# Moving the strip loads of a three-group encoder kernel from SyncE's queue to GpSimd's

## The chip, the cores and the metric

The kernel runs on one core of one Trainium2 chip. A core has five engines with a queue of instructions each: TensorE (PE in the profile; its weight loads are shown as PEld), VectorE (DVE), ScalarE (ACT), GpSimd (POOL) and SyncE (SP). Each engine takes its instructions strictly in the order of its queue and waits on semaphores for the others. Transfers run on 16 DMA engines that all queues share; an instruction in the queue of SP, ACT or POOL starts each transfer.

The metric is the device time of one execution in microseconds (us), as a median over runs; lower is better.

## What is computed

The reference is a trunk of two layers on 256 tokens of width 2048 (`x`) with 256 memory tokens (`mem`), all in float32. Cut to what matters here:

```python
for l in range(DEPTH):                                   # DEPTH = 2
    h = rmsnorm(x, norm_g[l])
    proj = h @ w_in[l]                                   # 2048 x 7168
    a_x, a_b, a_c, a_g, d_q, d_k, d_v, d_g, m_q, m_g = split(proj)
    y_a = short_gated_conv(a_x, a_b, a_c, ...) * silu(a_g)
    y_d = diff_attention(...) * silu(d_g)
    mkv = rmsnorm(mem, mem_norm_g[l]) @ w_mem_kv[l]      # 2048 x 1024
    mk, mv = rmsnorm(mkv[..., :512] by head, mem_k_norm_g[l]), mkv[..., 512:]
    y_m = memory_attention(rmsnorm(m_q by head), mk, mv) * silu(m_g)
    x = x + concat(y_a, y_d, y_m) @ w_out[l]
```

## The kernel before

Every large product is made of three matmuls on PE: each operand is split into a high part rounded to PE's fast float32 format and a low part that holds the rest (high times high, high times low, low times high). ACT makes the high part, DVE the low part. The left operand must have the 2048 input columns on the partitions, so `mem`, `x` and all that follows is also needed turned.

**The memory stage comes first.** It computes `mkv` of both layers, 32 steps `s` in all: layer `l = s // 16`, and chunk `k = s % 16` of 128 of the 2048 input rows. A step loads one 128x1024 tile of `w_mem_kv` (`Memory.load`, L783, four `raw` buffers, SP's queue), splits it with the norm's gain (`Memory.make`, L793 on ACT and L794 on DVE, four buffers), and does twelve 128x512 matmuls in two halves, keys and values (`Memory.times`, L818 through L311). The loop at L905 runs the steps in order; the last two and the first two of a layer go as a group. `beside(s)` (L866) puts other work beside the steps. After a layer's last steps ACT copies the keys out of the accumulators (`kraw`, L894) and the values (`mv`, L899).

**How `mem` and `x` are turned.** Chunks 0 to 7 of `mem` are turned by PE (`rows_T`, L628). Chunks 8 to 15 of `mem` (two quarters, `m.columns`, L830) and all four quarters of layer 0's `x` (`x_turned`, L655) go another way: `strips_by_rows` (L639) loads a quarter of 512 columns as eight transfers of 64 KB, 512 bytes to a row, into a tile `xt` of the pool tag `e`, which has two buffers; DVE turns the tile in 32x32 blocks (`turn_strips`, L651) into `xf`; `split_T` (L267 and L268 for `memT`, L270 and L271 for `xT` with the gain `gx`) makes the two parts of the chunks. These transfers are issued from SP's queue, four and four, with the loads of weights between them. For `x` the four quarters are begun beside the steps k = 1, 4, 7 and 10 of layer 1.

**Small constants** (`load_constants`, L98) come on POOL's queue: four lambda vectors, `norm_g` into `gx`, and nine pieces into `vb`, in three parts beside k = 11, 12 and 13 of layer 0, held back by a copied column of `ssm` (L102). `rest_of_constants` (L154) works them out beside k = 8 of layer 1. POOL's queue also carries the keys' way through DRAM (`keys`, L744 out and L745 back), once for each layer.

**The order** of all that carries `keep_in_program_order` or `pin` is the order in which the program writes it; the rest is placed by a scheduler that works on a simulated time line. Generators in `tasks` yield the number of steps after which they go on (`later`, `run_side`).

Behind the memory stage come the blocks of each layer: `block` (L315) loads `w_in` or `w_out` tile by tile (L297), splits it (L300 on ACT, L301 on DVE) and multiplies (L311). The first block of layer 0 begins when its accumulators are free, that is, when L894 has copied the last keys.

Of the kernel before, what the change touches and what calls it, by code (L numbers as in the profile page):

```python
# [18 lines left out]
P = 128  # L19
# [29 lines left out]
def encoder(ctx: ExitStack, tc: tile.TileContext, x, mem, norm_g, w_in, conv_w, conv_b,  # L49
# [21 lines left out]
    def nm(s):  # L71
        uid[0] += 1
        return f"{s}_{uid[0]}"
# [24 lines left out]
    def load_constants(part):  # L98

        pin = tc.keep_in_program_order  # L100
        if part == 0:
            pin(nc.gpsimd.tensor_copy(vb[:, 0:NT], ssm[0:64, :, 3]))  # L102
            pin(nc.gpsimd.memset(vb, 0.0))
            for j, v in enumerate((lq1, lk1, lq2, lk2)):
                pin(nc.gpsimd.dma_start(lam_in[:, j, :], on_all_rows(v)))
        else:
            if part == 1:
                pin(nc.gpsimd.dma_start(gx.rearrange("p (m j) -> p m j", j=QT),
                                        norm_g.rearrange("l (q p j) -> p (l q) j", p=P, j=QT)))
            for r0, v in vb_rows[(part - 1) * 4:part * 4]:  # L110
                n, w = v.shape
                for j in range(P // w):
                    pin(nc.gpsimd.dma_start(vb[r0:r0 + n, j * w:(j + 1) * w], v))


    zeros = tmp.tile([P, NB], mybir.dt.bfloat16, tag="eT", name="zeros")
    nc.vector.memset(zeros, 0.0)
# [102 lines left out]
    def later(g, n):  # L220
        due[id(g)] = chunk[0] + n
        return g
# [399 lines left out]
    def rows_T(src, k, n):  # L622

        pt = ps_t.tile([P, 2, SEQ], F32, tag="t", name=nm("pt"))
        for j in range(n):
            for t in range(NT):
                tc.keep_in_program_order(
                    nc.tensor.transpose(pt[:, j, t * P:(t + 1) * P], src(k + j, t), ident))  # L628
        return [pt[:, j, :] for j in range(n)]

    def strips_of(src):

        st = tmp.tile([P, SEQ // B, B * QT], F32, tag="e", name=nm("xt"))
        for b in range(NA):
            tc.keep_in_program_order(nc.sync.dma_start(
                st[b * B:(b + 1) * B], src[:, b * B * QT:(b + 1) * B * QT].rearrange("(n p) r -> p n r", p=B)))
        return st

    def strips_by_rows(src):  # L639

        st = tmp.tile([P, SEQ // B, B * QT], F32, tag="e", name=nm("xt"))
        for n in range(SEQ // B):
            tc.keep_in_program_order(nc.sync.dma_start(  # L643
                st[:, n], src[n * B:(n + 1) * B].rearrange("p (b r) -> b p r", b=NA)))
            if n == SEQ // B // 2 - 1:
                yield 1
        return st

    def turn_strips(st):
# [2 lines left out]
                                                     st.rearrange("p n (c j) -> p j n c", j=QT)))  # L652
        return whole

    def x_turned(dst, l, q, src):  # L655

        if l == 0:
            st = yield from strips_by_rows(src)
            yield 3
        else:  # L660
            st = strips_of(src)
            yield 2
        whole = turn_strips(st)
        yield
        for j in range(QT):
            split_T(dst, q * QT + j, whole[:, j], g_norm(l, q * QT + j), pin=True)
            if j % 2:
                yield
# [97 lines left out]
    class Memory:  # L766
# [61 lines left out]
                split_T(memT, q * QT + j, self.strips[q][:, j], None, pin=True)  # L828

        def columns(self, q):  # L830
            self.strips[q] = yield from strips_by_rows(mem[:, q * NB:(q + 1) * NB])

    mkT, mv, stm, away = [], [], [], []
    m = Memory()
# [25 lines left out]
    m.begin(1, 0, 0)  # L860
    m.begin(1, 1, 0)
    m.begin(1, 0, 1)
    m.make(2)
    m.split(2, rows_T(mem_columns, 2, 2))

    def beside(s):  # L866

        l, k = divmod(s, KT)
        if l == 0:
            if k in (3, 5):  # L870
                m.split(k + 1, rows_T(mem_columns, k + 1, 2))
            if k in (3, 6):
                tasks.append(later(m.columns({3: 2, 6: 3}[k]), 0))
            if k in (6, 9):
                mem_tokens({6: 2, 9: 3}[k] * NB, NB)
            if k in (6, 7, 10, 11):
                m.turned(2 if k < 10 else 3, k % 2)
            if k in (2, 4, 8, 11):
                mem_squares((2, 4, 8, 11).index(k))
            if k == 11:  # L880
                tasks.append(later(mem_stats(), 1))
            if k in (11, 12, 13):
                load_constants(k - 11)
        else:
            if k == 8:
                rest_of_constants()
            if k in (1, 4, 7, 10):
                q = k // 3
                tasks.append(later(x_turned(xT, 0, q, x[:, q * NB:(q + 1) * NB]), 1))

    def keep_keys(l):
        kraw = keep.tile([P, NT, NB], F32, tag="ga", name=nm("kraw"))
# [12 lines left out]
    while s < DEPTH * KT:  # L905
        l, k = divmod(s, KT)
        group = (s, s + 1) if k in (KT - 2, 0) else (s,)
        for i in group:
            beside(i)
        for i in range(s, group[-1] + 3):  # L910
            m.make(i)
        for half in range(2):
            for i in group:
                m.times(i, half)
            if k == KT - 2:
                (keep_keys, keep_values)[half](l)
        for i in group:
            for ahead in range(i + 1, i + 5):
                m.load(ahead)
            run_side(1)  # L920
        s = group[-1] + 1
# [201 lines left out]
```

## Time and profile before

| what | value |
|---|---|
| median of 3 runs | 940.33 us (939.9 to 941.63) |
| the profiled execution, as a run | 942.95 us |
| its span in the profile | 940.8 us |
| mean granted clock of TensorE | 0.995 |
| busy: PE, DVE, ACT, POOL | 924.4, 672.9, 494.7, 14.8 us |
| issues of L643 (strips) on SP | 48, of 64 KB each |
| issues from POOL's queue | 24: 4 lambda vectors, `norm_g`, 9 of `vb`, 8 of `kd`, 2 back |

The profile comes from one execution. A row of the time line gives the start, the duration, the engine, the line of the kernel, the operation, what it writes and reads, the number of instructions merged in the row, and in brackets how long the engine had been idle before and what ended that. `SPq` marks the issue of a transfer, not the transfer itself. Rows of the chain of waits give start, duration, and what held the end back at that time.

### The profile page before, as it was taken

How to read it: one execution, taken by the hardware profiler on the slowest of the kernel's cores; microseconds unless marked ns; L12 is line 12 of the kernel's file. 1: busy time of each engine (PE TensorE's matmuls, PEld its weight loads, DVE VectorE, ACT ScalarE, POOL GpSimd, SP SyncE). 2: the span in 40 equal slices, each digit the busy share in tenths (PEclk: the TensorE clock that was granted, in tenths of full speed). 3: DMA queues.
4: the chain of work that ended last, by engine and by line, in shares of the span. 5: the costliest groups of instructions: out<-in, count | busy, mean ns of one | idle time of the engine just before them, and what ended most of it. 6: DMA issues, size and time to landing. Idle time of an engine off the chain costs nothing.

```text
span 940.8 us, 12267 instructions
## 1 busy us (share of the span) xinstructions
PE 924.4 (98%) x4159; PEld 763.2 (81%) x4159; DVE 672.9 (72%) x1179; ACT 494.7 (53%) x751; POOL 14.8 (2%) x33
## 2 busy tenths in 40 slices
PE   9889799999999999999999999999999999999998
PEld 6678588888888888888888888888888888888886
DVE  5667687866789686556767766887898776558652
ACT  6554564568455454435555544568654554446331
POOL 0031010000000000000000000000000000000000
PEclk9999899999999999999999999999999999999999
DMA  7777887886677999998678866886888989988762
GB/s 256 236 218 214 295 266 216 235 242 208 181 222 197 245 265 244 248 273 246 208 245 256 259 198 186 232 259 186 245 222 221 253 224 246 254 238 238 221 210 81
DMA packets 250765, 216.09 MB, mean 230 GB/s; under 512 B 130266, under 2 KB 177160, under 8 KB 250704
## 3 DMA queue, kind: packets, MB, share of 16 engines
q1 hardware_dynamic: 248416, 211.86, 77.9%
q0 software_dynamic: 1120, 2.41, 1.0%
q10 hardware_dynamic: 1168, 1.07, 0.4%
q8 instruction: 32, 0.52, 0.2%
q14 instruction: 29, 0.24, 0.1%
HBM read 194.31 MB, written 20.97 MB: 229 GB/s over the span
## 4 chain that ended last, share of the span: by engine, by line
PE 89%; DMA 4%; ACT 3%; DVE 2%; issue 1%; SPq 0%; DVEq 0%; ACTq 0%
PE acc L311 84%; DMA raw<-in_w_mem_kv_dram 4%; PE po L451 2%; ACT hi L793 2%; DVE lo L794 1%; DVE xf L651 1%; PE s L604 1%; PE s L559 1%; PE s L558 1%; SPq L643 0%; ACT msq L718 0%; PE acc L807 0%; PE warm L122 0%; ACT memT L267 0%; ACT sq L368 0%
## 5 line engine op out<-in xcount | busy, mean ns | idle before, releaser
L311 PE MATMUL acc<-hi,xT 128*128 128x512 f32 x1792 | 563.1, 392 | 2.8 <-ACT kraw L894 2.8
L300 ACT CAST hi<-raw 128x1024 fp32r<-128x1024 f32 x288 | 302.7, 1052 | 346.2 <-PE acc L311 290.7
L301 DVE TENSOR_TENSOR lo<-raw,hi 128x1024 fp32r<-128x1024 f32 x288 | 351.6, 1222 | 184.9 <-ACT hi L300 180.1
L311 PEld LDWEIGHTS acc<-hi,xT 128*128 128x128 f32 x1792 | 337.8, 189 | 72.7 <-ACT kraw L894 3.2
L311 PE MATMUL acc<-lo,xT 128*128 128x512 f32 x896 | 350.1, 391 | 0.0
L311 PEld LDWEIGHTS acc<-lo,xT 128*128 128x128 f32 x896 | 169.0, 189 | 34.3
L311 PE MATMUL acc<-hi,yT 128*128 128x512 f32 x512 | 158.0, 389 | 0.0
L311 PEld LDWEIGHTS acc<-hi,yT 128*128 128x128 f32 x512 | 96.1, 188 | 19.9
L311 PE MATMUL acc<-lo,yT 128*128 128x512 f32 x256 | 99.6, 389 | 0.0
L311 PE MATMUL acc<-hi,memT 128*128 128x512 f32 x248 | 79.2, 399 | 6.4 <-ACT hi L793 4.0
L311 PEld LDWEIGHTS acc<-hi,memT 128*128 128x128 f32 x248 | 47.1, 191 | 18.0 <-ACT hi L793 5.7
L794 DVE SCALAR_TENSOR_TENSOR lo<-raw,cva,hi 128x1024 fp32r<-128x1024 f32 (+1 forms) x34 | 41.4, 1221 | 22.0 <-ACT hi L793 22.0
L311 PEld LDWEIGHTS acc<-lo,yT 128*128 128x128 f32 x256 | 48.0, 188 | 10.1
L311 PE MATMUL acc<-lo,memT 128*128 128x512 f32 x124 | 48.7, 400 | 2.1 <-DVE lo L794 1.8
L793 ACT ACTIVATE hi<-raw,cva 128x1024 fp32r<-128x1024 f32 (+1 forms) x34 | 36.7, 1097 | 24.1 <-DMA raw<-in_w_mem_kv_dram 20.5
L311 PEld LDWEIGHTS acc<-lo,memT 128*128 128x128 f32 x124 | 23.7, 191 | 9.2 <-DVE lo L794 4.5
L569 ACT ACTIVATE e<-e,mx 128x256 f32<-128x256 f32 x48 | 23.8, 499 | 1.4 <-DVE mx L565 1.3
L651 DVE STREAM_TRANSPOSE xf<-xt 128x1024 f32<-128x1024 f32 x10 | 20.0, 2004 | 3.6 <-DMA raw<-in_w_mem_kv_dram 3.2
L270 ACT ACTIVATE xT<-xf,gx 128x256 fp32r<-128x256 f32 x32 | 14.5, 500 | 8.6 <-DVE xf L651 6.6
L413 DVE STREAM_TRANSPOSE sh<-sh 128x1024 f32<-128x1024 f32 (+2 forms) x14 | 17.3, 1234 | 0.0
L563 DVE SCALAR_TENSOR_TENSOR e<-dist,s 128x512 f32<-128x512 f32 x24 | 15.7, 678 | 2.2 <-PE s L559 1.7
L1084 DVE TENSOR_TENSOR xs<-acc,xs 128x256 f32<-128x256 f32 (+1 forms) x24 | 10.8, 503 | 7.8 <-PE acc L311 7.8
(159 smaller groups left out, 543.4 us busy)
## 6 DMA issues: line engine op xcount, KB each, us to landing
raw<-in_w_in_dram SPq DMA_DIRECT2D x192, 512.0 KB
raw<-in_w_out_dram SPq DMA_DIRECT2D x64, 512.0 KB
raw<-in_w_in_dram SPq DMA_DIRECT2D x64, 256.0 KB
raw<-in_w_mem_kv_dram SPq DMA_DIRECT2D x30, 512.0 KB
d<-sh SPq DMA_DIRECT2D x80, 128.0 KB
sh<-d SPq DMA_DIRECT2D x64, 128.0 KB
d<-yn SPq DMA_DIRECT2D x40, 64.0 KB
yn<-d SPq DMA_DIRECT2D x40, 64.0 KB
```

Of the source, the lines that this page charges most:

```text
L270: both = (nc.scalar.activation(hi, src, AF.Copy, scale=gain), nc.vector.scalar_tensor_tensor(lo, src, gain, hi.bitcast(F32), ALU.mult, ALU ...
L300: nc.scalar.copy(hi, raw)
L301: nc.vector.tensor_tensor(lo_, raw, hi.bitcast(F32), ALU.subtract)
L311: i = nc.tensor.matmul(acc, left, right, start=start, stop=stop)
L413: tc.keep_in_program_order(nc.vector.transpose(src, src))
L451: nc.tensor.matmul(po[:, t, :], eT[:, i, t, k, :], v[:, k, h * P:(h + 1) * P], start=k == 0, stop=k == NT - 1)
L563: nc.vector.scalar_tensor_tensor(e[:, c], dist, -slopes[h], s[c], ALU.mult, ALU.add)
L569: nc.scalar.activation(e[:, c, i], e[:, c, i], AF.Exp, bias=mx[:, c, i:i + 1], accum_out=sm[:, c, i:i + 1])
L651: tc.keep_in_program_order(nc.vector.transpose(whole.rearrange("p j (n i) -> p j n i", i=B), st.rearrange("p n (c j) -> p j n c", j=QT)))
L793: both = (nc.scalar.activation(hi[:, j], raw[:, j], AF.Copy, scale=g), nc.vector.scalar_tensor_tensor(lo[:, j], raw[:, j], g, hi[:, j].bit ...
L794: nc.vector.scalar_tensor_tensor(lo[:, j], raw[:, j], g, hi[:, j].bitcast(F32), ALU.mult, ALU.subtract))
L1084: nc.vector.tensor_tensor(xc, acc[t][:, lo:lo + n], xc, ALU.add)
```

## The change

1. `strips_by_rows` issues its eight transfers from POOL's queue, without a break after four. It can be given `after`: POOL then first copies one column of that tensor into the tile, and since the transfers write the same tile, they wait for the copy, which waits for its source.
2. The two quarters of `mem` wait in this way for one chunk of `memT` (chunk 5 for quarter 2, chunk 9 for quarter 3); quarter 3 is begun beside k = 7 and not 6. The first quarter of `x` waits for the memory's statistics (`stm`); the others have no copied column.
3. The quarters of `x` are begun beside k = 2, 3, 6 and 9 of layer 1 (before 1, 4, 7, 10), with waits of 3, 5, 5 and 5 steps until they are turned, so that the turning stands beside k = 5, 8, 11 and 14.
4. `norm_g` is loaded by a function of its own beside k = 9 of layer 0, held back by a copied column of `ssm`. The other constants come beside k = 4, 5 and 6 of layer 1, behind the first two quarters of `x` on POOL's queue, without a copied column; `rest_of_constants` goes from k = 8 to k = 11.
5. At the start, chunk 2's split of weights and the turning of chunks 2 and 3 stand within step 1 and not ahead of it, and step 1 makes the weights of steps 1 and 2 alone.

In the order that results, ACT has, ahead of the last copy of keys (`kraw`), the third cast of `w_in` and four `xT` casts; the scaling of `mkT` comes later than the copy. DVE has the last transpose of `x` behind the seventh split of `w_in` tiles.

```diff
@@ load_constants
         if part == 0:
-            pin(nc.gpsimd.tensor_copy(vb[:, 0:NT], ssm[0:64, :, 3]))
             pin(nc.gpsimd.memset(vb, 0.0))
...
-            if part == 1:
-                pin(nc.gpsimd.dma_start(gx.rearrange("p (m j) -> p m j", j=QT),
-                                        norm_g.rearrange("l (q p j) -> p (l q) j", p=P, j=QT)))
...
+    def load_norm():
+
+        tc.keep_in_program_order(nc.gpsimd.tensor_copy(gx[:, 0:NT], ssm[:, :, 1]))
+        tc.keep_in_program_order(nc.gpsimd.dma_start(gx.rearrange("p (m j) -> p m j", j=QT),
+                                                     norm_g.rearrange("l (q p j) -> p (l q) j", p=P, j=QT)))
...
-    def strips_by_rows(src):
+    def strips_by_rows(src, after=None):
 
         st = tmp.tile([P, SEQ // B, B * QT], F32, tag="e", name=nm("xt"))
+        if after is not None:
+            tc.keep_in_program_order(nc.gpsimd.tensor_copy(st[:, 0, 0:1], after))
         for n in range(SEQ // B):
-            tc.keep_in_program_order(nc.sync.dma_start(
+            tc.keep_in_program_order(nc.gpsimd.dma_start(
                 st[:, n], src[n * B:(n + 1) * B].rearrange("p (b r) -> b p r", b=NA)))
-            if n == SEQ // B // 2 - 1:
-                yield 1
         return st
...
-    def x_turned(dst, l, q, src):
-
-        if l == 0:
-            st = yield from strips_by_rows(src)
-            yield 3
-        else:
-            st = strips_of(src)
-            yield 2
+    def x_turned(dst, l, q, src, after=None, wait=2):
+
+        st = strips_of(src) if l else strips_by_rows(src, after)
+        yield wait
...
         def columns(self, q):
-            self.strips[q] = yield from strips_by_rows(mem[:, q * NB:(q + 1) * NB])
+            self.strips[q] = strips_by_rows(mem[:, q * NB:(q + 1) * NB], memT[:, 0, 4 * q - 3, 0:1].bitcast(F32))
...
     m.begin(1, 0, 1)
-    m.make(2)
-    m.split(2, rows_T(mem_columns, 2, 2))
...
-            if k in (3, 6):
-                tasks.append(later(m.columns({3: 2, 6: 3}[k]), 0))
+            if k in (3, 7):
+                m.columns({3: 2, 7: 3}[k])
...
+            if k == 9:
+                load_norm()
             if k == 11:
                 tasks.append(later(mem_stats(), 1))
-            if k in (11, 12, 13):
-                load_constants(k - 11)
         else:
-            if k == 8:
+            if k in (4, 5, 6):
+                load_constants(k - 4)
+            if k == 11:
                 rest_of_constants()
-            if k in (1, 4, 7, 10):
+            if k in (2, 3, 6, 9):
                 q = k // 3
-                tasks.append(later(x_turned(xT, 0, q, x[:, q * NB:(q + 1) * NB]), 1))
+                tasks.append(later(x_turned(xT, 0, q, x[:, q * NB:(q + 1) * NB], stm[0][:, R, 0:1] if q == 0 else None,
+                                            (3, 5, 5, 5)[q]), 0))
...
-        for i in range(s, group[-1] + 3):
+        for i in range(s, group[-1] + (2 if s == 1 else 3)):
             m.make(i)
         for half in range(2):
             for i in group:
                 m.times(i, half)
+            if s == 1 and half == 0:
+                m.split(2, rows_T(mem_columns, 2, 2))
```

## The prediction

> **What bounds the kernel now.** I read the page's first lines, then busy time by stretch, then the waits on TensorE (PE), and last the SyncE queue (SP) in the stretches where PE stood still.
>
> ```profile
> span 940.8 us, 12267 instructions
> PE 924.4 (98%) x4159; PEld 763.2 (81%) x4159; DVE 672.9 (72%) x1179; ACT 494.7 (53%) x751; POOL 14.8 (2%) x33
> ```
>
> PE sets the end, so an edit to transfers can only win where PE stands still or runs slowly. The view of stretches finds those places. Its columns: stretch, length, then busy time and instruction count of PE, PEld, DVE, ACT and POOL, granted clock, DMA share, GB/s.
>
> ```profile
> 31.40:45.20 13.80, 11.51 (x49) 8.86 (x48) 9.21 (x11) 8.12 (x15) 0.00 (x0) 1.00 0.74 239
> 45.20:59.40 14.20, 11.63 (x48) 8.78 (x48) 10.86 (x24) 8.86 (x15) 8.06 (x16) 1.00 0.80 235
> 59.40:95.50 36.10, 36.09 (x157) 29.19 (x157) 26.03 (x49) 18.17 (x25) 2.81 (x5) 1.00 0.70 215
> 95.50:110.20 14.70, 11.10 (x37) 7.69 (x36) 11.63 (x13) 5.89 (x9) 0.00 (x0) 0.88 0.77 247
> 110.20:113.10 2.90, 0.14 (x1) 0.00 (x0) 1.22 (x1) 2.90 (x6) 0.00 (x0) 0.87 1.05 390
> 113.10:118.90 5.80, 5.78 (x14) 4.52 (x15) 4.68 (x11) 5.80 (x11) 0.00 (x0) 0.50 0.99 340
> 118.90:200.00 81.10, 81.10 (x359) 67.13 (x358) 66.17 (x130) 45.66 (x61) 2.74 (x5) 1.00 0.82 238
> ```
>
> The third row is PE at its pace: 36.10/157 = 0.230 us per matmul. Against that, length minus count x 0.230 gives what each stretch loses: 13.80 - 49 x 0.230 = 2.5 us, 14.20 - 48 x 0.230 = 3.2, then 14.70 - 37 x 0.230 = 6.2, then 2.9, then 5.80 - 14 x 0.230 = 2.6. That is 17.4 us, all in the memory stage and the first step behind it; from 118.9 on PE is full. So 17.4 us, 1.8%, is all that can be won. PE's own rows name what it waited for:
>
> ```profile
> 32.77 1.20 PE L311 MATMUL acc<-hi,memT 128*128 128x512 f32 x4 [1.33 <-ACT hi L793]
> 45.29 1.20 PE L311 MATMUL acc<-hi,memT 128*128 128x512 f32 x4 [0.93 <-ACT hi L793]
> 59.41 0.50 PE L311 MATMUL acc<-hi,memT 128*128 128x512 f32 x1 [2.37 <-ACT kraw L894]
> 103.26 0.50 PE L311 MATMUL acc<-hi,memT 128*128 128x512 f32 x1 [1.42 <-ACT hi L793]
> 113.12 0.79 PE L311 MATMUL acc<-hi,xT 128*128 128x512 f32 x1 [2.77 <-ACT kraw L894]
> ```
>
> **Part A, the late weights at 95.5 to 110.2.** SP's queue beside VectorE's (DVE's) splits, which free the raw buffers, and the chain of waits:
>
> ```profile
> 83.83 3.46 SPq L643 DMA_DIRECT2D xt<-in_x_dram  x4
> 87.39 2.88 SPq L783 DMA_DIRECT2D raw<-in_w_mem_kv_dram  x2
> 90.36 4.25 SPq L643 DMA_DIRECT2D xt<-in_x_dram  x4
> 94.71 2.37 SPq L783 DMA_DIRECT2D raw<-in_w_mem_kv_dram  x1
> ```
>
> ```profile
> 79.17 1.28 DVE L794 SCALAR_TENSOR_TENSOR lo<-raw,cva,hi 128x1024 fp32r<-128x1024 f32 x1 [0.30 <-ACT hi L793]
> 87.18 1.28 DVE L794 SCALAR_TENSOR_TENSOR lo<-raw,cva,hi 128x1024 fp32r<-128x1024 f32 x1
> ```
>
> ```profile
> 94.71 7.25 DMA raw<-in_w_mem_kv_dram
> 102.06 1.16 ACT hi L793
> ```
>
> Four raw buffers turn round. The split at 79.17 frees one at 80.45, yet its load is issued only at 87.39, behind four strip issues (83.83 to 87.29). The split at 87.18 frees another at 88.46; its load goes out at 94.71, behind four more (90.36 to 94.61), takes 7.25 us, and ScalarE (ACT) can cast only at 102.06: PE's 1.42 us wait at 103.26. The two loads are some 6 us late by SP's order alone. With no strip on SP, the turn is: split ends, 7.25 us of transfer, 1.16 cast, 1.28 split, together 9.7 us, against 4 chunks x 12 matmuls x 0.230 = 11.0 us that PE needs for four chunks. So weights should stay ahead: **-6.2 us**. Bounds 0 (the DMA engines, not SP, make them late) and -6.2.
>
> **Part B, the step to layer 0 at 110.2.** The next accumulators wait until ACT has copied the keys:
>
> ```profile
> 109.70 1.05 ACT L300 CAST hi<-raw 128x1024 fp32r<-128x1024 f32 x1 [1.64 <-PE acc L311]
> 110.66 1.15 ACT L751 ACTIVATE mkT<-mkT,mgain 128x1024 f32<-128x1024 f32 x1
> 111.71 0.89 ACT L270 ACTIVATE xT<-xf,gx 128x256 fp32r<-128x256 f32 x2
> 112.50 1.04 ACT L894 COPY kraw<-acc 128x512 f32<-128x512 f32 x2
> ```
>
> Two instructions stood between the cast and the copy. In the changed order of ACT they become four xT casts (2 x 0.89), and the scaling of mkT goes behind. The cast waits for the buffer of PE's last chunk but one, whose last six matmuls end 6 x 0.230 = 1.4 us before the stage does; then 1.05 + 1.8 + half of 1.04 = 3.4 us, so PE stands 2.0 us instead of 2.9: **-0.9**. Bounds -2.9 and +1. The clock behind it was 0.50 and cost 2.6 us. An idle 2.37 us at 59.41, behind full work, was followed by 1.00; the 2.77 us at 113.12 came behind a stretch already at 0.88. With Part A gone the new gap resembles the first: I take **-2.6**, bounds 0 and -2.6. [...]
>
> **Part C, the memory strips, now issued by GpSimd (POOL).** In the trace the two strips end thus, with the ACT casts that will gate them in the changed kernel:
>
> ```profile
> 18.79 0.37 ACT L267 CAST memT<-pt 128x256 fp32r<-128x256 f32 x1 [1.10 <-DVE memT L268]
> 28.92 1.99 DVE L651 STREAM_TRANSPOSE xf<-xt 128x1024 f32<-128x1024 f32 x1 [2.01 <-DMA raw<-in_w_mem_kv_dram]
> 30.95 0.71 ACT L267 CAST memT<-xf 128x256 fp32r<-128x256 f32 x2 [5.36 <-DVE xf L651]
> 41.46 1.98 DVE L651 STREAM_TRANSPOSE xf<-xt 128x1024 f32<-128x1024 f32 x1 [1.22 <-DMA raw<-in_w_mem_kv_dram]
> ```
>
> The gates are memT chunk 5 (ends 19.16) and chunk 9 (ends 31.66). What POOL pays stands in its own rows; DMA sizes and medians to landing are from the view of issues:
>
> ```profile
> 47.14 0.18 POOL L102 COPY vb<-ssm 64x2 f32<-64x2 f32 x1 [45.35 <-ACT msq L718]
> 47.98 0.70 POOL L105 DMA_DIRECT2D lam_in<-in_lambda_q_dram  x1 [0.41 <-issue]
> 49.74 0.54 POOL L105 DMA_DIRECT2D lam_in<-in_lambda_k_dram  x1
> 56.31 0.51 POOL L113 DMA_DIRECT2D vb<-in_diff_head_norm_g_dram  x1 [1.18 <-DMA lam_in<-in_lambda_k_dram]
> ```
>
> ```profile
> lam_in<-in_lambda_k_dram POOLq DMA_DIRECT2D x2, 64.0 KB, 5.1
> sh<-kd POOLq DMA_DIRECT2D x2, 512.0 KB, 6.1
> vb<-in_mem_k_norm_g_dram POOLq DMA_DIRECT2D x1, 1.0 KB, 4.1
> ```
>
> A lam_in issue has a strip issue's shape: 64 KB into 128 partitions, 512 bytes each. A strip is eight of them: 0.70 + 7 x 0.54 = 4.5 us, plus 0.18 for the copy and 0.41 before the first. First strip: 19.16, plus 0.3 because that cast, too, moves behind squares, plus 0.6, plus 4.5 = 24.6; second: 31.66 + 0.3 + 8 x 0.54 = 36.3, both plus the landing. One row shows a landing of a 64 KB piece straight: issued by 50.28, waited for until 56.31, 6.0; its median is 5.1. I take 5.4, between them. So the transposes start at 30.0 and 41.7 instead of 28.92 and 41.46: **+1.1 and +0.2 us**, passed on in full, since DVE and ACT run in order and PE already waits there (32.77, 45.29). Bounds by the 4.1 and 6.1 rows: 28.7 to 30.7 and 40.4 to 42.4, so -1.3 to +2.7 together. The wait at 59.41 hangs on the chain behind the second strip and moves with it: 0.
>
> **Part D, the rest.** Chunk 1 now starts before chunks 2 and 3 are turned, which puts chunk 3's cast behind two squares: +0.2, bounds 0 and 1.2 (about one cast, 1.16 above). Layer 0's strips have these marks in DVE's rows: the statistics that gate the first, and the first and third transpose.
>
> ```profile
> 54.25 0.17 DVE L195 COPY stm<-rsy 128x2 f32<-128x2 f32 x1
> 72.50 1.98 DVE L651 STREAM_TRANSPOSE xf<-xt 128x1024 f32<-128x1024 f32 x1
> 97.08 1.99 DVE L651 STREAM_TRANSPOSE xf<-xt 128x1024 f32<-128x1024 f32 x1
> ```
>
> POOL's queue in order, at 0.54 an issue and 5.4 a landing, each issue waiting for the landing eight back: first strip 55 to 60, landed by 65; second 61 to 66; thirteen constants 67 to 76, landed by 81; third strip 77 to 82, landed by 88; the four key stores, for which POOL's read-back waits, to 87, read-back near 92; fourth strip 92 to 96, landed by 102. Needed: the first at 72.5, the third at 97, the constants in chunk 27, which PE ends at 59.4 + 12 chunks x 2.8 = 93, the fourth six chunks into layer 0, at 107 + 17 = 124. Each has 7 us of cover or more, so 0; without it the delay would count in full, since PE takes its work in order. The fourth transpose also stands in DVE's new order behind seven splits of w_in, so the last xT columns only just precede their matmuls: +0.5, bounds 0 and 3 (about one chunk).
>
> **Sum.** -6.2 - 0.9 - 2.6 + 1.3 + 0.2 + 0.5 = -7.7 us: a span of 933.1 for 940.8. That profiled execution took 942.95 us as a run; the median is 940.33, so the time is 940.33 - 7.7 = **932.6**.
>
> **The rivals.**
> - *The step stalls as before* (0.20). A gains, B does not: its copy is still behind four casts that need a strip turned just before. For: the order is still copy-last. Against: 2.37 us passed without a lower clock. 932.6 + 3.5 = 936.1.
> - *Strips come earlier* (0.17). On SP the strips stood behind weight loads; POOL has a queue of its own. At 4.1 us landing C is -1.3 rather than +1.3, and with no constants in flight at 47 to 57 a further 1.5 of the 2.37 us wait goes: 932.6 - 4.1 = 928.5. Against: POOL's landings beside weight loads took 5.1 to 6.0.
> - *The DMA engines were the bound* (0.13): weights are as late from POOL's traffic as from SP's order. For: 0.77 share and 247 GB/s where PE waited. Against: 0.70 and 215 where it did not, and 390 GB/s a moment later. A and B yield nothing: 940.33 + 2.0 = 942.3 at the worst, about 940 if the step alone is better.
> - *POOL's strips come late, slower than before* (0.10). Every us beyond 5.4 is paid at both strips. The 7.7 us are used up when each is 3.9 us late: a landing of 9.3 us, or an issue of 1.0 us for 0.54. At 11 us: 932.6 + 2 x 5.6 = 943.8. Against: no POOL landing here took over 6.1 by its median. [...]
>
> The forecast itself has 0.40. About 0.2% (1.9 us) is what a measurement of this kernel tells from no change. Faster by more: the forecast, the first two rivals and a little of the third, 0.80; within: most of the rest of the third, 0.09; slower: the fourth and a tail of the third, 0.11. The range is 926.5 to 940: below, C and D at their best and the wait at 59.41 gone; above, the third rival with the step improved.
>
> **What would show it.** Right: no strip issue in SP's queue; weight loads at 80 to 95 issued within a us of the split that frees them; a stage from 95 that runs at 0.230 per matmul; the first matmul on xT near 107.5 instead of 113.12, at clock 1.00; the two memory transposes at about 30 and 42. Wrong: ACT still waiting for raw in 82 to 102, a strip transpose beyond 33 or 45, PE standing at the vb transpose (constants late), or a second low clock at the step.

## The result, and the profile after

| | before | changed kernel |
|---|---|---|
| median of 5 runs each, side by side | 940.33 us (939.9 to 941.67) | 944.48 us (942.57 to 945.37) |
| ratio, 95% interval | | 1.0037 [1.0021, 1.0053] |
| the profiled execution: as a run, its span | 942.95, 940.8 us | 945.37, 943.5 us |
| mean granted clock | 0.995 | 0.989 |

The kernel became slower by 0.4%, where 932.6 us was forecast with a range up to 940. It went the way of the fourth rival, "POOL's strips come late, slower than before", to which the prediction gave 0.10.

The head of the changed kernel's page shows that PE's work is the same, and that its span is longer all the same:

```profile
span 943.5 us, 12283 instructions
PE 924.6 (98%) x4159; PEld 765.2 (81%) x4159; DVE 670.6 (71%) x1179; ACT 494.3 (52%) x751; POOL 49.2 (5%) x84
```

Next, the busy time by stretch of the changed kernel, with the columns that the prediction explains. Its last three stretches before 118.90 are the ones of before; others are cut where PE starts again after a wait:

```profile
5.70:31.40 25.70, 24.52 (x107) 19.09 (x106) 13.05 (x17) 12.96 (x24) 5.74 (x9) 1.00 0.84 264
...
39.58:46.20 6.62, 6.62 (x16) 5.22 (x17) 5.61 (x6) 4.91 (x9) 6.18 (x10) 0.53 0.68 191
...
57.37:63.70 6.33, 6.33 (x17) 5.01 (x18) 5.24 (x11) 5.71 (x10) 0.00 (x0) 0.57 0.40 136
...
59.40:95.50 36.10, 36.10 (x154) 29.70 (x153) 29.01 (x54) 21.13 (x25) 21.53 (x35) 0.95 0.89 245
95.50:110.20 14.70, 14.70 (x66) 11.88 (x65) 10.83 (x19) 7.69 (x10) 7.14 (x13) 1.00 0.98 307
...
116.96:119.00 2.04, 2.04 (x6) 1.64 (x7) 0.72 (x2) 2.04 (x4) 0.00 (x0) 0.63 1.10 221
119.00:121.00 2.00, 2.00 (x7) 1.55 (x6) 1.22 (x1) 2.00 (x5) 0.00 (x0) 0.53 1.07 217
```

PE's waits in the time line of the changed kernel (L313 is the L311 of before, L791 its L793, L893 its L894):

```profile
39.58 2.08 PE L313 MATMUL acc<-hi,memT 128*128 128x512 f32 x4 [6.89 <-ACT hi L791]
...
57.37 2.08 PE L313 MATMUL acc<-hi,memT 128*128 128x512 f32 x4 [3.72 <-ACT hi L791]
...
116.96 0.50 PE L313 MATMUL acc<-hi,xT 128*128 128x512 f32 x1 [1.90 <-ACT kraw L893]
```

The two halves of the change show here side by side. **The late part gained.** From 95.50 to 110.20, where PE lost 6.2 us before, it is busy 14.70 of 14.70 us, and the step to layer 0 costs 1.90 us instead of 2.77. **The early part lost more.** At the first matmuls of chunk 8 and of chunk 12, those that need a strip, PE waits 6.89 us (before 1.33) and 3.72 us (before 0.93), and behind each wait it works at about half the clock (0.53 and 0.57).

The sums, from these rows: in the memory stage 1.2 us at the start (25.70 - 24.52), 6.89 + 3.72 of waits, and by the clock 6.62 x 0.47 + 6.33 x 0.43 = 5.8 us; together 17.6, where the same stretches lost 2.5 + 3.2 = 5.7 before. At the step 1.90 us and by the clock 2.04 x 0.37 + 2.00 x 0.47 = 1.7; together 3.6, where 6.2 + 2.9 + 2.6 = 11.7 were lost from 95.50 on. So +11.9 and -8.1, or +3.8 us; the spans differ by 2.7 and the medians by 4.15. Such sums are good to a us or two: the pace of 0.230 us per matmul that the prediction takes from before is 14.70/66 = 0.223 in the full stretch here.

**Why the strips are late.** POOL's queue, from the time line of the changed kernel (L645 is the copied column, L647 an issue):

```profile
20.47 0.18 POOL L645 COPY xt<-memT 128x1 f32<-128x1 f32 x1 [18.67 <-ACT memT L269]
20.96 5.56 POOL L647 DMA_DIRECT2D xt<-in_mem_dram  x8 [0.31 <-POOL xt L645]
38.54 0.47 POOL L645 COPY xt<-memT 128x1 f32<-128x1 f32 x1 [12.02 <-ACT memT L269]
39.30 5.35 POOL L647 DMA_DIRECT2D xt<-in_mem_dram  x8 [0.29 <-POOL xt L645]
```

The casts on ACT and the transposes on DVE around it, from the same time line:

```profile
20.03 0.37 ACT L269 CAST memT<-pt 128x256 fp32r<-128x256 f32 x1 [1.59 <-DVE memT L270]
...
35.75 1.98 DVE L653 STREAM_TRANSPOSE xf<-xt 128x1024 f32<-128x1024 f32 x1 [7.61 <-DMA xt<-in_mem_dram]
...
37.77 0.71 ACT L269 CAST memT<-xf 128x256 fp32r<-128x256 f32 x2 [10.94 <-DVE xf L653]
...
53.54 1.98 DVE L653 STREAM_TRANSPOSE xf<-xt 128x1024 f32<-128x1024 f32 x1 [7.58 <-DMA gx<-in_norm_g_dram]
```

The first hold opens at 20.4, the eight issues end at 26.52, and the strip can be turned at 35.75, 9.2 us after the last issue. The second hold is the cast of chunk 9, which itself comes out of the first strip's turning (37.77, with DVE's xf as releaser); so the second strip is issued only from 39.30 to 44.65 and turned at 53.54, 8.9 us on. (The releaser named there is the load of `norm_g`, which POOL issued right behind the strip.) In the kernel before, the second strip did not wait for the first. Its time line of SP shows both halves of the second strip's issue, the first half at 26.10, ahead of the first strip's turning at 28.92:

```profile
26.10 3.85 SPq L643 DMA_DIRECT2D xt<-in_mem_dram  x4
...
32.58 2.92 SPq L643 DMA_DIRECT2D xt<-in_mem_dram  x4
```

Where the first strip's time went shows in the view of transfers of the changed kernel between 19 and 39 us. The digits are the busy tenths of the 16 DMA engines in slices of 0.5 us, the row below the GB/s; the last column of the issues is the median from issue to landing:

```profile
DMA  3799886786869898999999999988832110000000
GB/s 41 98 385 418 205 172 205 295 313 149 124 164 295 304 334 246 345 305 219 190 218 276 255 248 240 264 205 279 279 115 98 74 41 0 0 0 0 0 0 0
...
raw<-in_w_mem_kv_dram SPq DMA_DIRECT2D x4, 512.0 KB, 7.9
xt<-in_mem_dram POOLq DMA_DIRECT2D x8, 64.0 KB, 8.1
xs<-in_mem_dram SPq DMA_DIRECT2D x1, 512.0 KB, 9.2
```

Until 33.5 us the engines are busy, mostly at eight and nine tenths, with weights and a quarter of the tokens (xs), which SP, free of strips, issues as soon as buffers allow; a 64 KB piece of a strip takes as long as a 512 KB load of weights (8.1 and 7.9 us). The same view for 26.52 to 35.75, from the strip's last issue to its turning, gives 1.58 MB to the queue of SP and 0.36 MB to that of POOL. Then, from 36 on, nothing moves at all (a share of 0.00 from 36 to 39 us): the weights ahead have filled their buffers, PE and SP wait for the strip's turning (6.89 and 12.6 us), and the second strip, which could use the idle engines, is held back.

### The profile page after: what moved, and what is told of

The parts are those of the page before. It is cut to its first block, busy times and chain, and to the rows that moved or that the text cites. A ratio compares the mean times of both kernels' runs of the same rounds, so it can differ in the third digit from the quotient of the medians.

```text
span 943.5 us, 12283 instructions
## 1 busy us (share of the span) xinstructions
PE 924.6 (98%) x4159; PEld 765.2 (81%) x4159; DVE 670.6 (71%) x1179; ACT 494.3 (52%) x751; POOL 49.2 (5%) x84
## 3 DMA queue, kind: packets, MB, share of 16 engines
q10 hardware_dynamic: 1168, 1.07, 0.4%
## 4 chain that ended last, share of the span: by engine, by line
PE 94%; issue 2%; DMA 1%; POOL 1%; ACT 1%; DVE 1%; DVEq 0%; ACTq 0%; POOLq 0%
PE acc L313 89%; PE po L453 2%; POOL xt L647 1%; DMA gx<-in_norm_g_dram 1%; PE s L606 1%; PE s L561 1%; PE s L560 1%; DMA raw<-in_w_mem_kv_dram 0%; ACT hi L791 0%; PE warm L124 0%; PE acc L805 0%; DVE lo L792 0%; DVE xf L653 0%; ACT xT L272 0%; PE pva L137 0%
## 5 line engine op out<-in xcount | busy, mean ns | idle before, releaser
L313 PE MATMUL acc<-hi,xT 128*128 128x512 f32 x1792 | 562.2, 392 | 1.9 <-ACT kraw L893 1.9
L313 PEld LDWEIGHTS acc<-hi,xT 128*128 128x128 f32 x1792 | 337.2, 188 | 71.8 <-ACT kraw L893 2.3
L313 PE MATMUL acc<-lo,xT 128*128 128x512 f32 x896 | 349.3, 390 | 0.0
L313 PEld LDWEIGHTS acc<-lo,xT 128*128 128x128 f32 x896 | 168.8, 188 | 33.9
L313 PE MATMUL acc<-hi,yT 128*128 128x512 f32 x512 | 158.0, 389 | 0.0
L313 PEld LDWEIGHTS acc<-hi,yT 128*128 128x128 f32 x512 | 96.1, 188 | 20.1
L313 PE MATMUL acc<-lo,yT 128*128 128x512 f32 x256 | 99.6, 389 | 0.0
L313 PE MATMUL acc<-hi,memT 128*128 128x512 f32 x248 | 81.4, 411 | 10.6 <-ACT hi L791 10.6
L313 PEld LDWEIGHTS acc<-hi,memT 128*128 128x128 f32 x248 | 49.0, 200 | 22.0 <-ACT hi L791 11.4
L313 PEld LDWEIGHTS acc<-lo,yT 128*128 128x128 f32 x256 | 48.1, 188 | 9.8
L313 PE MATMUL acc<-lo,memT 128*128 128x512 f32 x124 | 49.5, 407 | 1.2 <-DVE lo L792 1.2
L791 ACT ACTIVATE hi<-raw,cva 128x1024 fp32r<-128x1024 f32 (+1 forms) x34 | 36.6, 1096 | 18.7 <-DMA raw<-in_w_mem_kv_dram 9.4
L313 PEld LDWEIGHTS acc<-lo,memT 128*128 128x128 f32 x124 | 24.4, 197 | 7.5 <-DVE lo L792 2.3
L647 POOL DMA_DIRECT2D xt<-in_x_dram x32 | 21.6, 682 | 5.6 <-DMA xt<-in_x_dram 3.4
L415 DVE STREAM_TRANSPOSE sh<-sh 128x1024 f32<-128x1024 f32 (+2 forms) x14 | 17.3, 1235 | 0.0
```

The source lines that it names most:

```text
L313: i = nc.tensor.matmul(acc, left, right, start=start, stop=stop)
L415: tc.keep_in_program_order(nc.vector.transpose(src, src))
L647: tc.keep_in_program_order(nc.gpsimd.dma_start(st[:, n], src[n * B:(n + 1) * B].rearrange("p (b r) -> b p r", b=NA)))
L791: both = (nc.scalar.activation(hi[:, j], raw[:, j], AF.Copy, scale=g), nc.vector.scalar_tensor_tensor(lo[:, j], raw[:, j], g, hi[:, j].bit ...
```

## The experiments

Each was profiled once and, unless said otherwise, timed in runs alternating with the kernel before, whose median was 940.41, 941.84 and 941.16 us on the three occasions (experiments 1 to 4, 5 to 8, 9 and 10). Differences between kernels are taken from their ratios to it, and are good to about 2 us. The diffs are against the changed kernel. Theory 1, formed on the result, was that the strips of `mem` on POOL cost the time and that the strips of `x` on POOL gain; theory 2 laid the loss elsewhere in the change.

**1. Only the strips of `mem` back on SP**, as they were issued before.

```diff
-            self.strips[q] = strips_by_rows(mem[:, q * NB:(q + 1) * NB], memT[:, 0, 4 * q - 3, 0:1].bitcast(F32))
+            self.strips[q] = yield from strips_on_sp(mem[:, q * NB:(q + 1) * NB])
...
-            if k in (3, 7):
-                m.columns({3: 2, 7: 3}[k])
+            if k in (3, 6):
+                tasks.append(later(m.columns({3: 2, 6: 3}[k]), 0))
```

> The changed kernel with the two strips of mem back on SP's queue, four and four beside k = 3 and 6 without a copied column; x's strips and the constants stay on POOL. Theory 1 (all of the loss is in the two memory strips, which on POOL are begun late and travel beside weights that SP now issues at once): transposes at about 29 and 41.5, PE waits there of at most 1.5 us, weights never late in 60 to 110, first matmul on xT at 106 to 109, time 930 to 934 us. Theory 2 (POOL's transfers as such, x's strips and constants too, make weights late): transposes the same, but ACT waits for raw in 60 to 110 and the time is 938 to 941.

936.47 us, ratio 0.9957 [0.9943, 0.9971]. PE's waits in its time line:

```profile
35.18 2.04 PE L313 MATMUL acc<-hi,memT 128*128 128x512 f32 x4 [2.61 <-ACT hi L801]
```

The wait at chunk 8 is 2.61 instead of 6.89 us, that at chunk 12 is gone, and the rest of the change gains 4 us over the kernel before. With the strips of `mem` on SP the loss is gone, so theory 2 falls, though the time is 2.5 us above what theory 1 expected: the first wait is longer than the 1.33 us of before. SP's queue in this kernel gives a reason:

```profile
18.75 2.45 SPq L655 DMA_DIRECT2D xt<-in_mem_dram  x4
```

Before, the first strip's first four transfers went out at 16.57. They stand behind a load of weights, which waits until a split frees its buffer; with the start of the change that split ends at 18.3 (before 16.16). The strip is turned at 31.35 instead of 28.92. So the moved start delays the strip when SP issues it.

**2. Only the strips of `x` back on SP**, at the steps of before; `mem` stays on POOL.

```diff
-        st = strips_of(src) if l else strips_by_rows(src, after)
-        yield wait
+        if l == 0:
+            st = yield from strips_on_sp(src)
+            yield 3
...
-            if k in (2, 3, 6, 9):
+            if k in (1, 4, 7, 10):
```

> The changed kernel with x's four strips back on SP's queue at the steps of before; the strips of mem stay on POOL with their holds. Theory 1: PE waits of 6 to 8 and 3 to 4 us stay at chunks 8 and 12, and the late weights near the end of the memory stage come back in part: 947 to 951 us. Theory 2: without x's strips on POOL most of the loss goes: 940 to 942.

952.34 us, ratio 1.0123 [1.0108, 1.0137]. From PE's time line, with the waits that ended on ACT:

```profile
37.95 2.08 PE L313 MATMUL acc<-hi,memT 128*128 128x512 f32 x4 [5.65 <-ACT hi L805]
55.46 2.07 PE L313 MATMUL acc<-hi,memT 128*128 128x512 f32 x4 [4.59 <-ACT hi L805]
...
112.64 0.96 PE L313 MATMUL acc<-hi,memT 128*128 128x512 f32 x3 [1.43 <-ACT hi L805]
...
122.52 0.79 PE L313 MATMUL acc<-hi,xT 128*128 128x512 f32 x1 [4.85 <-ACT kraw L906]
```

Late weights and the long step are back, on top of the two waits for the strips of `mem`: 8 us worse than the whole change (1.0123 less 1.0037), and 1.3 above the range of theory 1. With the rest of the change (start and constants) in both, the strips of `mem` on POOL alone thus cost 11.9 us, those of `x` alone gain 4.0 (experiment 1); both together give +4.1 and not +7.9. The parts don't add up. A late memory stage also gives the transfers behind it more time; that this is the reason was not shown.

**3. The holds opened earlier**: the strips of `mem` wait for chunks 1 and 5 of `memT` instead of 5 and 9, and begin beside k = 1 and 3. All strips stay on POOL.

```diff
-            self.strips[q] = strips_by_rows(mem[:, q * NB:(q + 1) * NB], memT[:, 0, 4 * q - 3, 0:1].bitcast(F32))
+            self.strips[q] = strips_by_rows(mem[:, q * NB:(q + 1) * NB], memT[:, 0, 4 * q - 7, 0:1].bitcast(F32))
...
-            if k in (3, 7):
-                m.columns({3: 2, 7: 3}[k])
+            if k in (1, 3):
+                m.columns({1: 2, 3: 3}[k])
```

> The changed kernel with the memory strips held back by chunks 1 and 5 of memT instead of 5 and 9, all still on POOL (first issue near 9 and 21 instead of 21 and 39). Theory 1 with the hold as its cause: at 9 to 10 us from issue to landing the strips are there by 25 and 36, PE waits at chunks 8 and 12 of under 1.5 us, less up to 2 us lost at the start to company there: 929 to 934 us. If the late landing is POOL's path as such (issue 0.68 us, landing 9 us whatever the hold, more at the busy start), waits of 3 us and more stay: 938 to 942.

931.75 us, ratio 0.9903 [0.9889, 0.9918]; repeated on the third occasion, 931.59 us, 0.9893 [0.9877, 0.991]. This is the version that beats both. Its POOL queue and DVE's transposes in the time line:

```profile
10.05 5.56 POOL L647 DMA_DIRECT2D xt<-in_mem_dram  x8 [0.31 <-POOL xt L645]
...
22.37 5.34 POOL L647 DMA_DIRECT2D xt<-in_mem_dram  x8 [0.32 <-POOL xt L645]
...
29.46 1.98 DVE L653 STREAM_TRANSPOSE xf<-xt 128x1024 f32<-128x1024 f32 x1
...
39.60 1.98 DVE L653 STREAM_TRANSPOSE xf<-xt 128x1024 f32<-128x1024 f32 x1
```

No bracket stands behind the transposes: the strips are there when DVE comes to them, and PE has no wait at chunks 8 and 12. The landing is not shorter than in the changed kernel: the median of both strips' pieces, from issue, is 8.0 us (there 7.7), and it is covered now. The same transfers in the same queue, issued 11 and 17 us earlier, turn +4 into -9 us. Its stretches show where:

```profile
5.70:31.40 25.70, 24.72 (x104) 19.56 (x104) 15.09 (x18) 13.15 (x24) 12.38 (x20) 1.00 0.93 273
31.40:45.20 13.80, 13.69 (x60) 10.71 (x59) 10.88 (x15) 10.32 (x22) 0.00 (x0) 1.00 0.85 264
45.20:59.40 14.20, 14.20 (x64) 11.78 (x63) 11.82 (x26) 10.70 (x14) 6.62 (x10) 1.00 0.75 223
59.40:95.50 36.10, 36.10 (x161) 29.57 (x160) 28.01 (x48) 17.75 (x21) 20.55 (x36) 1.00 1.01 270
95.50:110.20 14.70, 11.33 (x44) 8.98 (x43) 7.44 (x11) 9.35 (x18) 5.39 (x8) 0.88 1.07 301
```

The memory stage loses 1.0 + 0.1 = 1.1 us for 5.7 before, the weights of layer 1 come in time (36.10 of 36.10), and the one wait left, 14.70 - 11.33 = 3.4 us, is that at the step:

```profile
98.69 1.05 ACT L302 CAST hi<-raw 128x1024 fp32r<-128x1024 f32 x1 [1.51 <-DMA raw<-in_w_in_dram]
100.86 1.71 ACT L272 ACTIVATE xT<-xf,gx 128x256 fp32r<-128x256 f32 x4 [1.12 <-DVE xf L653]
102.47 1.05 ACT L893 COPY kraw<-acc 128x512 f32<-128x512 f32 x2
...
103.09 0.80 PE L313 MATMUL acc<-hi,xT 128*128 128x512 f32 x1 [3.37 <-ACT kraw L893]
```

The copy of the keys stands behind the four `xT` casts, and these wait 1.12 us for the transpose of the third quarter. On DVE it comes behind the split of the second `w_in` tile, whose cast waited 2.25 us for its load:

```profile
97.11 1.22 DVE L303 TENSOR_TENSOR lo<-raw,hi 128x1024 fp32r<-128x1024 f32 x1 [1.74 <-ACT hi L302]
...
98.81 2.02 DVE L653 STREAM_TRANSPOSE xf<-xt 128x1024 f32<-128x1024 f32 x1 [0.16 <-issue]
```

With the clock, 14.70 x 0.12 = 1.8, the late part loses 5.2 for 11.7. That is -4.6 and -6.5 us; the spans differ by 930.1 - 940.8 = -10.7.

**4. The start of before** (the fifth point of the change undone).

```diff
     m.begin(1, 0, 1)
+    m.make(2)
+    m.split(2, rows_T(mem_columns, 2, 2))
...
-        for i in range(s, group[-1] + (2 if s == 1 else 3)):
+        for i in range(s, group[-1] + 3):
...
-            if s == 1 and half == 0:
-                m.split(2, rows_T(mem_columns, 2, 2))
```

> The changed kernel with the start as before (chunk 2's split of weights and the turning of chunks 2 and 3 ahead of step 1, chunk 3 made in step 1). The first copied column then goes at about 19.3 instead of 20.5, and PE's waits for splits at 14 and 18 us go. If the later hold is passed on: 942.5 to 943.5 us. If the start is hidden behind the strip: 944 to 945.

945.18 us, ratio 1.0046 [1.003, 1.0062], the same as with the change. POOL's first copy begins at 20.21 instead of 20.47, PE's short waits for splits are gone, and both waits for the strips stay, 5.84 and 5.41 us. The start neither gains nor costs here.

**5. The holds of experiment 3 and the start of before.**

> The kernel with the earlier holds (chunks 1 and 5) and the start as before. PE's two waits for splits at 15 and 19 us (0.98 us together) go, if they come from the moved start: 930 to 931.5 us against 931.75. If the start is bound by the loads instead, 931.5 to 933.

931.55 us, 0.9892 [0.9874, 0.991], within the interval of experiment 3. PE's two waits for splits are gone, but it waits 0.75 us for tokens at 10.54 and 1.25 at chunk 8 instead. The result doesn't tell the two expectations apart: the start stays without an effect that these runs can see.

**6. Less traffic beside the first strip**: the load of a quarter of the tokens (512 KB) goes behind the first strip; the strips and their holds are untouched. This is a single profiled run.

```diff
-            if k in (6, 9):
-                mem_tokens({6: 2, 9: 3}[k] * NB, NB)
+            if k == 9:
+                mem_tokens(2 * NB, NB)
+                mem_tokens(3 * NB, NB)
...
-            if k in (2, 4, 8, 11):
-                mem_squares((2, 4, 8, 11).index(k))
+            if k in (2, 4, 10, 11):
+                mem_squares((2, 4, 10, 11).index(k))
```

> The changed kernel with the load of mem's third quarter by tokens (512 KB, issued at 23.2 beside the first strip) moved behind that strip's transpose (beside k = 9), its squares to k = 10. One look, for the first transpose. If the strip is late because it shares the DMA engines with SP's loads, 512 KB less at 260 GB/s lets it land about 2 us earlier: transpose at 33 to 34.3 instead of 35.75 and a first PE wait near 5 us. If POOL's path is slow by itself, 35.5 to 36 and 6.9. The second strip then has 1 MB of token loads beside it and may come later; the total is not the point.

From its time line:

```profile
20.12 5.56 POOL L647 DMA_DIRECT2D xt<-in_mem_dram  x8 [0.31 <-POOL xt L645]
...
32.20 1.98 DVE L653 STREAM_TRANSPOSE xf<-xt 128x1024 f32<-128x1024 f32 x1 [4.89 <-DMA xt<-in_mem_dram]
```

The last issue ends at 25.68 and the transpose starts 6.5 us later. In between SP's queue moved 1.13 MB instead of 1.58. In the changed kernel this landing took 9.2 us, but beside the same token load it took 8.0 us in experiment 2 and 7.3 in experiment 4. So only 0.8 us lies outside what single executions differ by: the direction is that of the traffic beside the strip, its size isn't shown. The whole is no faster (944.78 us for the one run): PE waits 4.17 us at the first strip, and the tokens now stand beside the second, where it waits 5.42.

**7. No holds**: neither strip has a copied column, and the first issue is at 1.50 us, the last of the sixteen at 17.3.

```diff
-            self.strips[q] = strips_by_rows(mem[:, q * NB:(q + 1) * NB], memT[:, 0, 4 * q - 3, 0:1].bitcast(F32))
+            self.strips[q] = strips_by_rows(mem[:, q * NB:(q + 1) * NB])
```

> The changed kernel without the copied columns of the two memory strips: POOL issues both at the program's start, 2 to 16 us. If only the late start costs, no PE wait stays at chunks 8 and 12 and the time is 930 to 933 us, as with the earlier hold. If the hold is needed to keep the first loads free, PE's first matmuls come 2 to 4 us later: 933 to 937.

935.69 us, ratio 0.9931 [0.9917, 0.9946]. Without holds the kernel beats before, but is some 3 to 4 us slower than experiments 3 and 5: the strips then run in the first microseconds beside the first weights, where their pieces take 9.3 us by the median from issue to landing (8.0 in experiment 3). From 5.70 to 31.40 PE loses 1.4 us and runs at 0.93 of its clock, and it waits 1.37 us at chunk 8. The transposes start at 32.77 and 42.91 instead of 29.46 and 39.60, neither waiting for its strip. A hold is of use; the two of the change open too late.

**8. Only the second hold opened earlier**: both strips wait for chunk 5, the second issued right behind the first.

```diff
-            if k in (3, 7):
-                m.columns({3: 2, 7: 3}[k])
+            if k == 3:
+                m.columns(2)
+                m.columns(3)
```

(The copied column is that of chunk 5 for both.)

> The changed kernel with both memory strips held by chunk 5 alone, the second issued right behind the first (from about 27 on instead of 39). If the second hold is a cause of its own, the second wait (3.7 us, and the low clock behind it, 2.9 us) goes and the first stays near 6.9: 936.5 to 939 us. If the second strip's company makes the first later in turn, a first wait of 8 us and more: 939 to 942.

937.57 us, ratio 0.9956 [0.994, 0.9972]. From its time line:

```profile
39.72 2.08 PE L313 MATMUL acc<-hi,memT 128*128 128x512 f32 x4 [6.57 <-ACT hi L791]
...
35.88 1.99 DVE L653 STREAM_TRANSPOSE xf<-xt 128x1024 f32<-128x1024 f32 x1 [7.29 <-DMA xt<-in_mem_dram]
46.02 1.98 DVE L653 STREAM_TRANSPOSE xf<-xt 128x1024 f32<-128x1024 f32 x1
```

The first wait stays, the second is gone. Of the 12.6 us between the change and experiment 3 (1.0037 less 0.9903), opening the second hold sooner brings 7.6 by itself (1.0037 less 0.9956), the first the rest.

**9. and 10. The copy of the keys at the step.** On top of experiment 3, other waits until the third and fourth quarters of `x` are turned, which changes ACT's order: `kraw` then stands right behind the second cast of `w_in`, ahead of the third cast and of the `xT` casts.

```diff
-                                            (3, 5, 5, 5)[q]), 0))
+                                            (3, 5, 4, 5)[q]), 0))
```

> The early holds of e3_hold_early, and the third quarter of x is turned 4 instead of 5 steps after its strip is begun. ScalarE's order changes: the copy of layer 1's keys (kraw) stands directly behind the second cast of w_in, ahead of the third cast and of the four xT casts. Theory (the step to layer 0 is set by what stands ahead of kraw on ScalarE, Part B): PE's wait for kraw falls from 3.37 us to 1.0 to 1.5 us (half of the copy's 1.04 and a semaphore), the clock behind it stays at 1.00, and the time is 929 to 930.5. Rival (PE is only made to wait a moment later, for the third cast of w_in or for the xT columns): as e3_hold_early, 931 to 932.5, with a wait for xT or hi in its place.

For the other kernel the waits are (3, 5, 7, 6):

> The early holds of e3_hold_early, and the third and fourth quarters of x are turned 7 and 6 instead of 5 steps after they are begun. The copy of the keys stands behind two casts of w_in, but the xT casts of the third quarter come behind the third cast of w_in and the last quarter's behind ten. Theory (Part B): PE's wait for kraw 1.0 to 1.5 us, time 929 to 930.5, if the later columns of xT are still ahead of their matmuls. Rival: the columns of the third quarter are late, a new wait for xT within layer 0's first block, 931 to 935.

And experiment 3 again beside them:

> The kernel of e3_hold_early again, so that the two variants are measured against it on the same chip: 930.5 to 932.5, a wait of about 3.4 us for kraw.

932.96 us, 0.9912 [0.9899, 0.9925], and 937.3 us, 0.996 [0.9947, 0.9972], beside 931.59 for experiment 3 again. The theory is right for the wait, which is gone from both kernels, and wrong for the time, which falls in neither. Of the rivals the first holds, half a us above its range. The second named the wrong wait: in the other kernel PE waits 4.68 and 2.87 us for parts of `w_in` tiles, not for `xT`, and the time is 2.3 us above its range. ACT and PE in the time line of the first:

```profile
96.59 1.06 ACT L893 COPY kraw<-acc 128x512 f32<-128x512 f32 x2
...
109.74 1.04 ACT L302 CAST hi<-raw 128x1024 fp32r<-128x1024 f32 x1 [4.41 <-DMA raw<-in_w_in_dram]
...
119.11 1.98 ACT L302 CAST hi<-raw 128x1024 fp32r<-128x1024 f32 x2
...
110.83 1.06 PE L313 MATMUL acc<-hi,xT 128*128 128x512 f32 x2 [2.21 <-ACT hi L302]
...
120.19 0.73 PE L313 MATMUL acc<-hi,xT 128*128 128x512 f32 x2 [1.71 <-ACT hi L302]
```

The keys are copied in time and PE no longer waits for them, but some 11 us after the step it waits 2.21 us for a tile of `w_in` that the DMA engines haven't brought. The wait of 1.71 us is another: no bracket stands behind the casts at 119.11, since ACT has worked without a break from 109.74 on, with squares of `xs` (L688) between its casts. In experiment 3 the fifth tile is cast at 110.26 without a wait for its load, and PE, which starts on `xT` 5.5 us later than here (103.09 for 97.58), finds it ready. From 95.50 to 110.20 the DMA engines stand at a share of 1.07 in experiment 3's row.

## Why the prediction was wrong

**The step that failed is the third term, Part C:** "First strip: 19.16, plus 0.3 ... plus 0.6, plus 4.5 = 24.6; second: 31.66 + 0.3 + 8 x 0.54 = 36.3, both plus the landing", with a landing of 5.4. It gave +1.3 us; the memory stage lost 11.9 more than before (0.2 of that was forecast in Part D). What the runs showed in its place:

- *The landing*, 9.2 and 8.9 us for 5.4, outside its bounds of 4.1 to 6.1. The rows behind it came from loads at 48 to 56 us, in company that was not that of the strips. In the changed kernel the strips run beside weights and tokens on busy engines (a share of 0.92 from 22 to 34 us): SP's queue moved 1.58 MB while the last 0.36 MB of the first strip came in. With 512 KB fewer beside it the first landed after 6.5 us (experiment 6), with all of it after 7.3 to 9.2 (experiments 2 and 4, the changed kernel). So how much of the 3.8 us is due to the company stays open. A queue of its own did not make the small pieces land sooner than the large loads beside them: 8.1 us for a strip's 64 KB, 7.9 for 512 KB of weights.
- *The issue*, 5.56 us a strip for 4.5: 0.68 each, not 0.54. The row at 47.98 had 0.70 for a first issue and I took the lower one for the rest.
- *The second hold*, opened at 38.54 instead of near 32. I read chunk 9's end from the time line of before, where it was fixed, and did not move it with the first strip, from which that chunk is made. So the first strip's delay is passed on to the second's issue. In the kernel before the second strip stood in SP's queue with no such tie. Experiment 8 takes this tie away alone and gains 7.6 us. Reckoned step by step, the first transpose is 35.75 - 30.0 = 5.8 us later than forecast (about 0.9 of hold, 1.0 of issue, 3.8 of landing), the second 53.54 - 41.7 = 11.8 (6.5 of hold, 1.8 of copy and issue, 3.5 of landing).
- *The clock behind the waits*, 5.8 us in the memory stage, was in no term. The granted clock was 0.53 and 0.57 behind the waits, and I had priced such a fall only at the step.

**Part A was right.** Weights in layer 1's chunks stay ahead: PE is full from 95.50 to 110.20, where it lost 6.2. That this isn't only because PE came there later is shown by experiment 3: PE comes to the step 13.9 us earlier (103.09 for 116.96) and is full until it stands there. Experiment 2, with the strips of `x` on SP, has the late weights again. The weights stay ahead only just: in the changed kernel ACT still waits for its load before the casts at 82.38, 86.05 and 101.37 (1.18, 2.52 and 1.46 us). The prediction had named that as a sign of being wrong, but PE does not wait for any of them.

**Part B was right for its wait, but only while the memory stage is late.** 1.90 us was measured for a forecast of 2.0, and the third cast of `w_in` starts when PE frees its buffer, at 113.78, 1.3 us before PE ends the stage (forecast 1.4). (Before, three instructions stood between the cast and the copy, not two, as the row at 111.71 counts two; the sum does not use that number.) In experiment 3, where the stage ends 15 us sooner, the same order on ACT gives 3.37, since the `xT` casts wait for a transpose that stands on DVE behind a late tile of `w_in`. The wait is 2.00 us in experiment 4, whose stage is as late, and 3.0 to 4.7 where the stage ends sooner (experiments 1, 5, 7 and 8). And experiments 9 and 10 show that a shorter wait there buys nothing: behind the step the loads of `w_in` bind first, which the third rival had for the whole of the late part. *The clock saving* of 2.6 was 0.9: the half clock still cost 1.7 us behind a wait of 1.90.

**Part D was right in what counts.** The start cost 1.2 us in its stretch for 0.2 forecast, which is the bound given, but experiment 4 finds no time in it; the strips and constants of `x` stalled nothing, so their cost of 0 holds.

What lies behind 95.50 was forecast at -6.2 - 0.9 - 2.6 + 0.5 = -9.2 us and measured at -8.1. **The fourth rival named the mechanism** and put the point from which it decides at a landing of 9.3 us; the landing was 9.2 and 8.9. It was given 0.10 because no median of POOL's landings was over 6.1, which was read at the wrong moment of the trace, and it, too, lacked the tie of the second strip to the first and the clock. By its own price, such landings give 932.6 + 3.8 + 3.5 = 939.9 us; the rest of the way to 944.5 lies in what it lacked.

What stays open: how much of the long landing is due to the traffic beside the strips, and whether the 1.3 us that experiment 1 waits longer at the first strip than the kernel before are all due to the moved start, since it was not tried with the start of before.

## What to carry to other kernels

When a transfer is moved to a queue of its own, it loses its place in the order of the old queue, and what stood behind it there can now run ahead of it and fill the DMA engines (here 1.58 MB of SP's queue beside the last 0.36 MB of a strip): price its landing from transfers made in that company (9.2 us here, for 5.4 assumed), and start it by as much sooner. A hold should wait for something that is finished early and does not depend on the transfer before it; otherwise the delays add up in a chain (5.8 us at the first transpose here, 11.8 at the second). When a wait is removed from a place, look whether the DMA engines there are full, since the next load may then take its place (in experiment 9 PE waited 2.21 us for a tile of `w_in`, behind a stretch at a share of 1.07).

## What was unexpected of the hardware

- The granted clock fell behind waits of very different length: behind 6.89 and 3.72 us in the changed kernel (0.53 and 0.57 over the next 6 us), and behind 1.90 us (0.63 and 0.53 over the next 4 us), but not behind the 2.37 us at 59.41 before (1.00 from there to 63). So the length of a wait does not decide alone; what else does, these traces do not show. What they do show is the price: 3.1 and 2.7 us behind the strips, 1.7 us at the step.
- The issue of a strip's 64 KB from POOL took 0.68 us, that of the 64 KB of a lambda vector 0.54, though both write 128 partitions of 512 bytes. The sources differ: the lambda load reads one row for all partitions; that this is the reason was not tried.
- The end of the first strip came in a trickle: from 33.5 to 35.5 us the engines were three tenths busy and less, at 115 to 41 GB/s, while DVE waited for the strip. By queue, 48 of the 60 packets from 33.5 on were SP's and 12 POOL's, so the last 12 packets of the strip took some 1.5 us on engines that were mostly idle (a share of 0.23 from 33.5 to 35.5 us).
